# Contrast adjustment of 48 images: first tile loaded as two DMAs with two pieces per row, and stored as one

## The chip, the cores and the metric

The kernel runs on one core of one Trainium2 chip. The metric is the device time of one execution in microseconds (us); 239.36 is the median of three runs, which lie between 239.26 and 239.40. Beside the runs there is a profile of one execution, from which all times of parts come.

## The reference

```python
def setup_inputs():
    batch, c, h, w = 16, 3, 512, 512
    return {"x": np.random.rand(batch, c, h, w).astype(np.float32), "factor": np.float32(1.5)}

def reference(x, factor):
    mean = np.mean(x, axis=(2, 3), keepdims=True)
    return np.clip(mean + factor * (x - mean), 0, 1).astype(np.float32)
```

There are 48 images (16 x 3) of 512 x 512 numbers. Each gets its own mean, and every number becomes factor * x + (1 - factor) * mean, cut to between 0 and 1. All of an image has to be read before any of it can be written.

## The kernel before, in words

The 50.33 MB of input are cut into 6 tiles. A tile has 128 partitions, and each partition holds one row of ROW = 16384 numbers (64 KB), so a tile is 8 MB and holds 8 images of 16 partitions each. A buffer in on-chip memory, `ring`, has room for three tiles (BUFS = 3). Tile t uses place t % 3, and the result overwrites the input there.

For each tile, `compute` does this:

- `add` forms the sum of each row in two parts at once. VectorE (DVE) sums the first SUM = 4352 columns with a tensor_reduce (L85), and ScalarE (ACT) the rest, with a copy in place that also accumulates (L89).
- TensorE (PE) multiplies these sums with `blockw` (L100). That matrix holds (1 - factor) / 262144 where two partitions belong to the same image, so each partition gets its image's shift. The result is one column of `bias`.
- DVE computes factor * x + shift in place (L103), then the clip (L106).
- `store` writes the tile out (L80).

All loads (L77) and stores (L80) are issued by SyncE (SP), in the order in which they are written, since the schedule is by hand. They go into one DMA queue that 16 DMA engines work off. A DMA over 128 rows gives each engine 8 rows, and a packet is one contiguous piece of a row. The order on SP is: loads of tiles 0, 1 and 2; stores of tiles 0, 1 and 2; loads of 3, 4 and 5; stores of 3, 4 and 5. A store waits on SP until L106 of its tile is done, and what stands behind it on SP waits as well. Load 3 waits until store 0 has landed, since they share a place in `ring`; so do load 4 for store 1 and load 5 for store 2.

Tile 0 is treated apart. It is loaded by three DMAs: columns 0 to 2048 (1 MB), 2048 to 8192 (3 MB) and 8192 to 16384 (4 MB). Its sums are formed by halves: four partial sums instead of two, with a reduction of 4352 and an activation of 3840 columns for each half, and four products with `blockw`. Its scaling and clip are cut at column 2048, and each of the two parts has a store of its own.

Of the kernel before, what the change touches and what calls it, by code (L numbers as in the profile page):

```python
# [1 line left out]

# [4 lines left out]


P = 128  # L10
ROW = 16384
HALF = ROW // 2
BUFS = 3
SHORT = 2048
SUM = 4352


@with_exitstack
def kernel(
    ctx: ExitStack,  # L20
    tc: tile.TileContext,
    x: bass.AP,
    factor: float,
    out: bass.AP,
):

    nc = tc.nc
    f32 = mybir.dt.float32  # L30
    Alu = mybir.AluOpType
    Act = mybir.ActivationFunctionType

    B, C, H, W = x.shape
    n_img, n_pix = B * C, H * W
    ppi = n_pix // ROW
    per_tile = P // ppi
    n_tiles = n_img // per_tile
    assert ppi * ROW == n_pix and per_tile * n_tiles == n_img

    factor = float(factor)
    wconst = (1.0 - factor) / float(n_pix)

    x_f = x.rearrange("b c h w -> (b c h w)")
    out_f = out.rearrange("b c h w -> (b c h w)")

    def dram(ap, t, c0=0, c1=ROW):
        return bass.AP(tensor=ap.tensor, offset=t * P * ROW + c0, ap=[[ROW, P], [1, c1 - c0]])

    consts = ctx.enter_context(tc.tile_pool(name="consts", bufs=1))  # L50
    xpool = ctx.enter_context(tc.tile_pool(name="xpool", bufs=1))
    small = ctx.enter_context(tc.tile_pool(name="small", bufs=1))
    psum = ctx.enter_context(tc.tile_pool(name="psum", bufs=1, space=bass.MemoryType.PSUM))


    sums = small.tile([P, 4 * n_tiles], f32, name="sums")
    bias = psum.tile([P, n_tiles], f32, name="bias")

    blockw = consts.tile([P, P], f32, name="blockw")
    blocks = blockw.rearrange("p (a b) -> p a b", b=ppi)  # L60
    nc.gpsimd.memset(blockw, wconst)  # L61
    for base, step in ((0, -ppi), (ppi - 1, ppi)):
        nc.gpsimd.affine_select(  # L63
            out=blocks,
            in_=blocks,
            compare_op=Alu.is_ge,
            fill=0.0,
            base=base,
            pattern=[[step, per_tile], [0, ppi]],
            channel_multiplier=1 if step < 0 else -1,  # L70
        )


    ring = xpool.tile([P, BUFS, ROW], f32, name="ring")

    def load(t, c0=0, c1=ROW):
        nc.sync.dma_start(out=ring[:, t % BUFS, c0:c1], in_=dram(x_f, t, c0, c1))  # L77

    def store(t, c0=0, c1=ROW):
        nc.sync.dma_start(out=dram(out_f, t, c0, c1), in_=ring[:, t % BUFS, c0:c1])  # L80

    def add(t, col, c0, c1, c2):
        xt = ring[:, t % BUFS, :]
        own = sums[:, 4 * t + col : 4 * t + col + 2]
        nc.vector.tensor_reduce(  # L85
            out=own[:, 0:1], in_=xt[:, c0:c1], axis=mybir.AxisListType.X, op=Alu.add
        )
        part = xt[:, c1:c2]
        nc.scalar.activation(out=part, in_=part, func=Act.Copy, accum_out=own[:, 1:2])  # L89
        return [own[:, 1:2], own[:, 0:1]]  # L90

    def compute(t, *cuts):
        xt = ring[:, t % BUFS, :]
        if t == 0:
            parts = add(t, 0, 0, SUM, HALF) + add(t, 2, HALF, HALF + SUM, ROW)
        else:
            parts = add(t, 0, 0, SUM, ROW)
        shift = bias[:, t : t + 1]
        for k, part in enumerate(parts):
            nc.tensor.matmul(shift, blockw, part, start=k == 0, stop=k == len(parts) - 1)  # L100
        for c0, c1 in zip((0, *cuts), (*cuts, ROW)):
            part = xt[:, c0:c1]
            nc.vector.tensor_scalar(  # L103
                out=part, in0=part, scalar1=factor, scalar2=shift, op0=Alu.mult, op1=Alu.add
            )
            nc.vector.tensor_scalar(  # L106
                out=part, in0=part, scalar1=0.0, scalar2=1.0, op0=Alu.max, op1=Alu.min
            )
            store(t, c0, c1)

    with tc.manual_schedule():
        load(0, 0, SHORT)
        load(0, SHORT, HALF)
        load(0, HALF, ROW)
        load(1)
        load(2)
        compute(0, SHORT)
        compute(1)
        compute(2)
        load(3)  # L120
        load(4)
        load(5)
        compute(3)
        compute(4)
        compute(5)


# [1 line left out]
_INS = ['x', 'factor']  # L129
_OUTS = [((16, 3, 512, 512), 'float32')]  # L130

_NUMBERS = {'factor': 1.5}


# [26 lines left out]
```

## Time and profile before

| what | us |
|---|---|
| median of the runs (lowest, highest) | 239.36 (239.26, 239.40) |
| profiled execution: span, from its first to its last instruction | 237.3 |
| median of the runs less that span | 2.06 |
| DVE busy | 137.4 |
| ACT busy | 59.9 |
| PE busy | 7.9 |

The profile gives no total for the profiled execution beside its span; what lies around the span is taken as the difference to the median of the other runs.

How to read the views: in the list of groups a row gives line, engine, operation, shapes and count, then busy time and the mean of one. In the timeline the first number is the start, the second the duration, and the bracket tells how long the engine was idle before and what ended that. The row of digits headed DMA shows the busy share of the 16 DMA engines in equal slices of the window, in tenths. The queue line gives packets, megabytes and the packets' time as a share of 16 engines' span. A DMA issue is listed with its size and the time from issue to landing. The packet records of the trace, from which some durations are taken, hold start, duration and size of every packet of every DMA; a DMA's last packet on each engine has 4 bytes and reports its completion.

### The profile page before, as it was taken

The page shows a single profiled execution, that of the slowest core. Times are in us where ns is not written, and L with a number is a line of the kernel's source. Part 1 is how long each engine was busy: PE and PEld are TensorE (multiplying, and loading weights), DVE is VectorE, ACT ScalarE, POOL GpSimd, SP SyncE. Part 2 cuts the span into 40 slices and gives each one's busy share as a digit, 9 for nine tenths or more (in the row PEclk, how much of TensorE's full clock was granted, in tenths as well). Part 3 has the DMA queues.
Part 4 walks back from the last instruction along what each step waited for, and adds up shares of the span by engine and source line. Part 5 has one row for each costly group of instructions (what it writes and reads, how often), then busy time and mean ns, then how long its engine had stood idle before and what let it go on. Part 6 is the DMA issues. An engine that isn't in the chain of part 4 may idle for free.

```text
span 237.3 us, 186 instructions
## 1 busy us (share of the span) xinstructions
PE 7.9 (3%) x28; PEld 6.9 (3%) x28; DVE 137.4 (58%) x21; ACT 59.9 (25%) x15; POOL 1.1 (0%) x7
## 2 busy tenths in 40 slices
PE   0010100010001000000000000100000000000000
PEld 0010100010001000000000000100000000000000
DVE  0071899949998998000000043499989998991000
ACT  2051300980492000000000049319509800000000
POOL 1000000000000000000000000000000000000000
DMA  7999989899799798989899998989899998989894
GB/s 289 418 442 442 530 353 530 353 486 398 331 464 454 341 530 353 530 353 519 365 442 442 398 486 353 530 354 530 353 475 409 431 453 376 508 353 530 353 530 177
DMA packets 2160, 100.66 MB, mean 424 GB/s; under 512 B 240, under 2 KB 240, under 8 KB 240
## 3 DMA queue, kind: packets, MB, share of 16 engines
q1 hardware_dynamic: 2160, 100.66, 98.7%
HBM read 50.33 MB, written 50.33 MB: 424 GB/s over the span
## 4 chain that ended last, share of the span: by engine, by line
DVE 43%; DMA 36%; ACT 9%; PE 2%; SPq 1%; issue 0%; DVEq 0%; ACTq 0%
DMA ring<-in_x_dram 36%; DVE ring L103 18%; DVE ring L106 18%; ACT ring L89 9%; DVE sums L85 6%; PE bias L100 2%; SPq L77 1%; SPq L80 0%; DVEq L103 0%; ACTq L89 0%
## 5 line engine op out<-in xcount | busy, mean ns | idle before, releaser
L89 ACT ACTIVATE ring<-ring 128x12032 f32<-128x12032 f32 (+1 forms) x7 | 58.0, 8280 | 128.2 <-DMA ring<-in_x_dram 128.2
L85 DVE TENSOR_REDUCE sums<-ring 128x1 f32<-128x4352 f32 x7 | 32.8, 4683 | 63.9 <-DMA ring<-in_x_dram 63.9
L103 DVE TENSOR_SCALAR ring<-ring,bias 128x16384 f32<-128x16384 f32 (+2 forms) x7 | 52.8, 7538 | 12.9 <-PE bias L100 12.9
L106 DVE TENSOR_SCALAR ring<-ring 128x16384 f32<-128x16384 f32 (+2 forms) x7 | 52.3, 7476 | 0.2
L100 PE MATMUL bias<-sums,blockw 128*128 128x1 f32 x28 | 7.9, 360 | 189.1 <-ACT ring L89 175.4
L100 PEld LDWEIGHTS bias<-sums,blockw 128*128 128x128 f32 x28 | 6.9, 314 | 190.0 <-ACT ring L89 159.4
L89 ACT ACT_TABLE_LOAD x1 | 1.3, 1283 | 0.8 <-PEq L142 0.8
L89 ACT ACTIVATION_READ_ACCUMULATOR ring<-ring 128x1 f32 x7 | 1.3, 187 | 0.0
L63 POOL TENSOR_SCALAR_AFFINE_SELECT blockw<-blockw 128x128 f32<-128x128 f32 x2 | 0.7, 340 | 0.1
L61 POOL MEMSET blockw<- 128x128 f32 x1 | 0.2, 204 | 0.3 <-POOLq L142 0.3
L142 POOL MEMSET const-bfloat16-1.0<- 128x1 bf16 x1 | 0.1, 102 | 0.0
L142 POOL MEMSET const-uint8-127<- 128x1 uint8 x1 | 0.1, 102 | 0.0
L142 POOL MEMSET const-float32-0.0<- 128x1 f32 x1 | 0.1, 98 | 0.3 <-issue 0.3
L142 POOL MEMSET const-float32-1.0<- 128x1 f32 x1 | 0.1, 98 | 0.0
## 6 DMA issues: line engine op xcount, KB each, us to landing
out_dram<-ring SPq DMA_DIRECT2D x1, 7168.0 KB, 35.9
ring<-in_x_dram SPq DMA_DIRECT2D x1, 4096.0 KB, 20.8
ring<-in_x_dram SPq DMA_DIRECT2D x1, 3072.0 KB, 11.6
ring<-in_x_dram SPq DMA_DIRECT2D x1, 1024.0 KB, 4.7
out_dram<-ring SPq DMA_DIRECT2D x1, 1024.0 KB, 34.3
ring<-in_x_dram SPq DMA_DIRECT2D x5, 57.7
out_dram<-ring SPq DMA_DIRECT2D x5, 27.0
```

The costliest lines, as they stand in the source:

```text
L61: nc.gpsimd.memset(blockw, wconst)
L63: nc.gpsimd.affine_select(out=blocks, in_=blocks, compare_op=Alu.is_ge, fill=0.0, base=base, pattern=[[step, per_tile], [0, ppi]], channel ...
L77: nc.sync.dma_start(out=ring[:, t % BUFS, c0:c1], in_=dram(x_f, t, c0, c1))
L85: nc.vector.tensor_reduce(out=own[:, 0:1], in_=xt[:, c0:c1], axis=mybir.AxisListType.X, op=Alu.add)
L89: nc.scalar.activation(out=part, in_=part, func=Act.Copy, accum_out=own[:, 1:2])
L100: nc.tensor.matmul(shift, blockw, part, start=k == 0, stop=k == len(parts) - 1)
L103: nc.vector.tensor_scalar(out=part, in0=part, scalar1=factor, scalar2=shift, op0=Alu.mult, op1=Alu.add)
L106: nc.vector.tensor_scalar(out=part, in0=part, scalar1=0.0, scalar2=1.0, op0=Alu.max, op1=Alu.min)
L142: nc = _bacc.Bacc("TRN2", target_bir_lowering=False, num_devices=1)
```

## The change

Tile 0 is now loaded by two DMAs. Each takes, from every row, one piece of both halves: the first takes columns 0 to 2048 and 8192 to 10240 (two pieces of 8 KB), the second 2048 to 8192 and 10240 to 16384 (two pieces of 24 KB). Each of the 16 DMA engines so gets 16 packets from each of the two. Tile 0 is then computed like every other tile: one reduction of 4352 columns, one activation of 12032, two products, one scaling and one clip over the whole row, and one store. The order of loads and stores of the tiles stays as it was. The numbers of the lines move: L85 becomes L92, L103 and L106 become L105 and L108, the stores' L80 becomes L87, and the two loads of tile 0 stand in L84.

```diff
-SHORT = 2048
+SHORT = ROW // 8
...
-    sums = small.tile([P, 4 * n_tiles], f32, name="sums")
+    sums = small.tile([P, 2 * n_tiles], f32, name="sums")
...
+    def load_first(c0, c1):
+        rows = bass.AP(
+            tensor=x_f.tensor, offset=c0, ap=[[ROW, P], [HALF, 2], [1, c1 - c0]]
+        )
+        halves = ring[:, 0, :].rearrange("p (a b) -> p a b", a=2)
+        nc.sync.dma_start(out=halves[:, :, c0:c1], in_=rows)
...
-    def compute(t, *cuts):
+    def compute(t):
         xt = ring[:, t % BUFS, :]
-        if t == 0:
-            parts = add(t, 0, 0, SUM, HALF) + add(t, 2, HALF, HALF + SUM, ROW)
-        else:
-            parts = add(t, 0, 0, SUM, ROW)
+        parts = add(t, 0, SUM, ROW)
...
-        for c0, c1 in zip((0, *cuts), (*cuts, ROW)):
-            part = xt[:, c0:c1]
-            nc.vector.tensor_scalar(
-                out=part, in0=part, scalar1=factor, scalar2=shift, op0=Alu.mult, op1=Alu.add
-            )
-            nc.vector.tensor_scalar(
-                out=part, in0=part, scalar1=0.0, scalar2=1.0, op0=Alu.max, op1=Alu.min
-            )
-            store(t, c0, c1)
+        nc.vector.tensor_scalar(
+            out=xt, in0=xt, scalar1=factor, scalar2=shift, op0=Alu.mult, op1=Alu.add
+        )
+        nc.vector.tensor_scalar(
+            out=xt, in0=xt, scalar1=0.0, scalar2=1.0, op0=Alu.max, op1=Alu.min
+        )
...
-        load(0, 0, SHORT)
-        load(0, SHORT, HALF)
-        load(0, HALF, ROW)
-        load(1)
-        load(2)
-        compute(0, SHORT)
-        compute(1)
-        compute(2)
-        load(3)
-        load(4)
-        load(5)
-        compute(3)
-        compute(4)
-        compute(5)
+        for first in range(0, n_tiles, BUFS):
+            turn = range(first, min(first + BUFS, n_tiles))
+            for t in turn:
+                if t == 0:
+                    load_first(0, SHORT)
+                    load_first(SHORT, HALF)
+                else:
+                    load(t)
+            for t in turn:
+                compute(t)
+                store(t)
```

More of the change, by code (lines that the diff above doesn't have):

```diff
@@ L11 @@
 ROW = 16384
+BUFS = 3
+SUM = 4352
 HALF = ROW // 2
-BUFS = 3
-SHORT = 2048
-SUM = 4352
+SHORT = ROW // 8
 @with_exitstack
@@ L77, in load, with add @@
         nc.sync.dma_start(out=ring[:, t % BUFS, c0:c1], in_=dram(x_f, t, c0, c1))
+    def load_first(c0, c1):
[4 more added lines that the diff above has]
+        nc.sync.dma_start(out=halves[:, :, c0:c1], in_=rows)
     def store(t, c0=0, c1=ROW):
         nc.sync.dma_start(out=dram(out_f, t, c0, c1), in_=ring[:, t % BUFS, c0:c1])
-    def add(t, col, c0, c1, c2):
+    def add(t, c0, c1, c2):
         xt = ring[:, t % BUFS, :]
-        own = sums[:, 4 * t + col : 4 * t + col + 2]
+        own = sums[:, 2 * t : 2 * t + 2]
         nc.vector.tensor_reduce(
```

## The prediction

> **What bounds the kernel now.** I read the page's queue line first, then the chain of waits, then the waits of SP, then the timeline of the first three tiles, and last the DMA activity in narrow windows.
>
> ```profile
> span 237.3 us, 186 instructions
> PE 7.9 (3%) x28; PEld 6.9 (3%) x28; DVE 137.4 (58%) x21; ACT 59.9 (25%) x15; POOL 1.1 (0%) x7
> DMA  7999989899799798989899998989899998989894
> q1 hardware_dynamic: 2160, 100.66, 98.7%
> ```
>
> The queue line is the one to see: there is one queue, and its packets fill 98.7% of the span on all 16 engines. No compute engine is above 58%. The chain of waits gives DVE 43% and DMA 36%, which would mislead here: it follows instructions back, and SP's instructions wait for DVE before they are issued.
>
> ```profile
> SPq L80 <- DVE ring L106: 181.8, 7, 47.8
> SPq L77 <- DMA out_dram<-ring: 25.6, 2, 19.3
> ```
>
> SP does wait 181.8 us for DVE, but each store it then issues joins a queue that is not empty. The DMA issues show it: a store needs far longer to land than its own data needs.
>
> ```profile
> out_dram<-ring SPq DMA_DIRECT2D x1, 7168.0 KB, 35.9
> out_dram<-ring SPq DMA_DIRECT2D x1, 1024.0 KB, 34.3
> ```
>
> The 1 MB store takes 34.3 us to land because two whole loads stand before it. So the kernel is one unbroken line of transfers: tiles 0, 1, 2 in, 0, 1, 2 out, 3, 4, 5 in, 3, 4, 5 out. What counts is the sum of the packets' times and any moment at which the line runs dry.
>
> Every DMA ends, on each engine, with a completion packet of 4 bytes. By the packet records of the trace the earliest of the 16 begins at 4.79, 12.06 and 21.74 us for the three loads of tile 0, at 41.06 and 61.40 for tiles 1 and 2, at 63.85 and 80.76 for the two stores of tile 0, then at 100.08, 119.40, 138.72, 158.04, 177.48, 196.79, 216.11 and 235.43. The differences are the prices: 7.27 us for a DMA of 24 KB rows, 9.68 for 32 KB rows, 2.45 for 8 KB rows (61.40 to 63.85, without the start of the run), 16.91 for 56 KB rows, 19.32 for a whole tile of 64 KB rows, read or written. The next DMA's first packet begins about 6 ns after the completion packet.
>
> **The change, part by part.**
>
> *First load.* Before: 2.45 + 7.27 + 9.68 = 19.40 us of queue. After: 16 packets of 8 KB per engine instead of 8, so 2 x 2.45, and 16 of 24 KB, so 2 x 7.27: 19.44. That is +0.04 us. I assume that a packet of 8 or 24 KB costs the same when its neighbour in the row lies 32 KB away; the bounds on that are in the next paragraph and in the rivals.
>
> *Start of the queue.* The first load is issued at 0.80 us and its first packet begins at 1.82, 1.02 us later; the 16 engines begin within 0.32 us of each other. The first DMA now has 256 pieces instead of 128. The five loads at the start are issued 0.46 us apart, so 128 pieces need at most 0.46 us. Lower end: 0, if the first packets go out while later pieces are still made (one could even gain the 0.32 us of spread if the pieces are dealt out differently, though nothing points there). Upper end: +1.02, if the whole lead doubles. I take 0, because SP's loads and stores, with rows from 8 to 64 KB, differ by more among themselves (327 to 622 ns to issue a load) than a count of pieces explains, and keep both ends. The second DMA's pieces are made beneath 4.9 us of the first one's packets.
>
> *First store.* Before 2.45 + 16.91 = 19.36 (61.40 to 80.76); after one DMA of 64 KB rows, 19.32: -0.04 us.
>
> *Later compute of tile 0.* This part looks costly and should cost nothing. Before, tile 0 is summed in halves and its first 1 MB is stored at 30.5 us:
>
> ```profile
> 12.86 3.40 ACT L89 ACTIVATE ring<-ring 128x3840 f32<-128x3840 f32 x1 [10.78 <-DMA ring<-in_x_dram]
> 22.58 3.40 ACT L89 ACTIVATE ring<-ring 128x3840 f32<-128x3840 f32 x1 [6.22 <-DMA ring<-in_x_dram]
> 30.41 7.68 DVE L103 TENSOR_SCALAR ring<-ring,bias 128x14336 f32<-128x14336 f32 x1
> 41.93 10.23 ACT L89 ACTIVATE ring<-ring 128x12032 f32<-128x12032 f32 x1 [15.86 <-DMA ring<-in_x_dram]
> 53.43 8.76 DVE L103 TENSOR_SCALAR ring<-ring,bias 128x16384 f32<-128x16384 f32 x1 [3.07 <-PE bias L100]
> ```
>
> After, both sums start when all of tile 0 is there, 22.58 + 0.04 = 22.62. A whole tile needs 11.50 us from ACT's start to L103 (41.93 to 53.43), then 17.48 for L103 and L106 (53.43 to 70.91): done at 51.60, store 0 issued at 51.7. DVE then sums tile 1: from the end of one tile to its next L103 it takes 5.35 (70.91 to 76.26), so L103 begins at 56.95 instead of 53.43, and store 1 goes out at 74.5 instead of 71.0. Tile 2 needs 22.85 (70.91 to 93.76): store 2 at 97.4 instead of 93.8, with load 3 right behind it on SP. With the 1.02 us lead the queue can take them at 52.7, 75.5 and 98.4. It asks for them when the transfer ahead ends: 61.40, 80.76 and 100.08. The margins are 8.7, 5.3 and 1.7 us; without this cover each microsecond too late would be one lost. Load 3 is asked for at 119.40, load 4 waits for store 1 (100.08) and load 5 for store 2, as before. So nothing from tile 3 on moves, and SP is not held on anything new: its wait for store 0 now has one DMA instead of two.
>
> *Fewer instructions.* One reduction, one activation, two matmul pairs and two tensor_scalar go. DVE, ACT and PE are off the path, so they give nothing.
>
> **Sum:** +0.04 - 0.04 + 0 = 0.00 us on the profiled span of 237.3. The median of the runs is 239.36, that is 2.06 us around the span, which no part of the change touches. Forecast 239.36.
>
> **The rivals.**
>
> *Faster: a stall goes with the small store.* One stretch of the line is too long: tile 2's load takes 20.34 us (41.06 to 61.40), all others 19.32 to 19.44. The packet records put it in the last packet of that load, on all 16 engines: 3.53 us on average instead of 2.42. At the second change from loads to stores (tile 5 to store 3) the last packets take 2.54. The DMA view in slices of 0.4 us shows both, first from 54 to 70 us, then from 172 to 188:
>
> ```profile
> DMA  0003900005900000002799999930039900099000
> ```
>
> ```profile
> DMA  0993000993000999000799000799000799000799
> ```
>
> Digits stand where packets end. In the first row the bursts come 2.4 us apart until 58 us, and the next one only after 61; in the second the beat goes on. What differs ahead of the stall is that an 8 KB store waits in the queue in the first case and a 64 KB one in the second. If that makes the stall, the change removes 3.53 - 2.54 = 0.99 us: 238.4. Against it: no store packet has begun yet, 8 KB and larger loads follow each other at the start without such a stall, and the first case is also the first write of the run at all, which the change keeps. The first read of the run is slow too (first packets 0.83 us instead of 0.31). I think the first write is the likelier owner: chance 0.25.
>
> *Faster: completions paid in series.* The last completion packets begin at 236.07 us at the latest and the span ends at 237.3, so a store's completion may cost up to 1.2 us; two DMAs fewer would then give 237.0 to 239.4. The 6 ns to the next DMA's packet speak against it: chance 0.02. The Trainium skill, "DMA: Bandwidth & Descriptors", section "Anatomy of one DMA — SWDGE (gpsimd) path", fits a fixed 2.0 us to each DMA of another issuing path; taken twice that would give 235.4. The trace disagrees for DMAs that stand in line.
>
> *Slower: the first load starts later.* If a DMA's first packet waits until all its pieces are made, 256 pieces lengthen the lead of 1.02 us by 0.46 (the issue spacing) up to 1.02, and since the line is never idle afterwards the end moves as much: 239.8 to 240.4, middle 240.1. It counts as slower from 0.48 us. For it: nothing hides the first 1.82 us. Against it: engines begin 0.32 us apart, so packets already go out one by one. Chance 0.13.
>
> *Slower: store 2 comes too late*, if DVE or ACT lose more than the 1.7 us of margin: 239.36 plus the overrun, for example 240.4. DVE's whole-tile operations repeat to 0.01 us, so 0.03. *The change does not do what it says*, the pieces go to few engines (two engines would need some 155 us for tile 0): the outer count is still 128, so 0.01.
>
> **How the numbers follow.** A difference under 0.2% (0.48 us) cannot be told from none. Same 0.56 (239.36, its own range 239.2 to 239.8 by half of the start's bound), faster 0.25 + 0.02 = 0.27, slower 0.13 + 0.03 + 0.01 = 0.17. The range has to reach the stall's case, 238.4 less 0.2 of spread, and the lower half of the later start: 238.2 to 239.9, which leaves out about 0.17.
>
> **What would show it.** Right: tile 0's completion packets end near 21.8 us, ACT waits for DMA until 22.6, store 0 is issued at 51.7 and lands near 82, and the stall before the first store is still 1.1 us. The stall's rival: a 64 KB last packet of load 2 near 2.5 us. The later start: a first packet after 2.2 us. Store 2 late: an empty slice near 99 us. Wrong altogether: 8 or 24 KB packets that are not 0.31 and 0.91 us long.

## The result, and the profile after

The changed kernel takes 242.01 us (median of four runs, 241.72 to 242.60), the kernel before 239.38 us beside it (239.26 to 239.53). The ratio is 1.011, with a 95% interval of 1.0098 to 1.0122: 2.63 us slower, where 239.36 was forecast. The profiled execution has a span of 240.4 us.

The page's lines that answer to those shown of before:

```profile
span 240.4 us, 169 instructions
PE 6.7 (3%) x24; PEld 5.9 (2%) x24; DVE 132.5 (55%) x18; ACT 63.2 (26%) x13; POOL 1.1 (0%) x7
DMA  6999989899898989898998989898999989898984
q1 hardware_dynamic: 2128, 100.66, 98.0%
```

The same bytes and a queue that is nearly as full, over a longer span. SP's waits do not explain it either:

```profile
SPq L87 <- DVE ring L108: 183.8, 6, 49.1
SPq L77 <- DMA out_dram<-ring: 20.7, 2, 19.4
SPq L87 <- DMA ring<-in_x_dram: 5.2, 1, 5.2
```

The last row is new, but it is a wait for tile 0's first load that ends at 8.5 us, long before store 0 is issued at 53.59. The packet records show where the time goes. The table sets the last completion packets of both traces side by side, for the slowest of the 16 engines, since the slowest sets the end.

| completion packet of | before, us | after, us | after less before |
|---|---|---|---|
| tile 0's load | 22.15 | 22.68 | +0.53 |
| load 2 (then the change to stores) | 62.02 | 62.36 | +0.34 |
| store 1 | 100.70 | 101.00 | +0.30 |
| store 2 (then the change to loads) | 120.02 | 120.78 | +0.76 |
| load 3 | 139.40 | 141.09 | +1.69 |
| load 4 | 158.72 | 160.41 | +1.69 |
| load 5 (then the change to stores) | 178.11 | 181.09 | +2.98 |
| store 5, the end | 236.07 | 239.05 | +2.98 |

So 0.30 us is left of a later start, and 2.7 us come at two changes of direction long after tile 0: from store 2 to load 3, and from load 5 to store 3. Between them nothing is lost; whole tiles take 19.32 us in both traces. The DMA activity shows it in slices of 0.4 us. First the kernel before, from 112 to 128 us:

```profile
DMA  9900009900009930009930009930009970009970
```

Then the changed kernel, from 112 to 128 us and from 172 to 188:

```profile
DMA  0990000990000990000099040039907039737009
```

```profile
DMA  3307973309995500099703399703399333399333
```

In the kernel before, the packets end in bursts 2.4 us apart all along. In the changed kernel's first row this beat breaks near 120 us: the third pause is longer, and afterwards single engines trail behind the burst. From 172 to 188 us the kernel before was regular too (shown with the prediction). In the changed kernel's second row the bursts are already spread out at its left end, there is a long pause near 178 us, and the trailing gets worse.

What is late ahead of the first of these places is store 2. The timeline of the changed kernel:

```profile
23.19 1.28 ACT L96 ACT_TABLE_LOAD   x1 [23.19 <-DMA ring<-in_x_dram]
24.48 10.23 ACT L96 ACTIVATE ring<-ring 128x12032 f32<-128x12032 f32 x1
36.04 8.76 DVE L105 TENSOR_SCALAR ring<-ring,bias 128x16384 f32<-128x16384 f32 x1 [8.14 <-PE bias L104]
99.28 0.33 SPq L87 DMA_DIRECT2D out_dram<-ring  x1
```

And of the kernel before, where the table load and store 2 stood:

```profile
0.80 1.28 ACT L89 ACT_TABLE_LOAD   x1 [0.80 <-PEq L142]
93.82 0.33 SPq L80 DMA_DIRECT2D out_dram<-ring  x1
```

ACT loads its function table before its first activation. In the kernel before that stands ahead of any wait and is done at 2.1 us. In the changed kernel the first activation waits for two DMAs; in ACT's instructions, in the order of the program, one of the two waits stands ahead of the table load and the other on the activation. So 1.28 us that used to be free stand on the path, and store 2 is issued at 99.28 us, 1.1 us before store 1's first completion packet at 100.41.

### The profile page after: what moved, and what is told of

It is laid out like the page before. It is cut to its first block, busy times and chain, and to the rows that moved or that the text cites. A ratio compares the mean times of both kernels' runs of the same rounds, so it can differ in the third digit from the quotient of the medians.

```text
span 240.4 us, 169 instructions
## 1 busy us (share of the span) xinstructions
PE 6.7 (3%) x24; PEld 5.9 (2%) x24; DVE 132.5 (55%) x18; ACT 63.2 (26%) x13; POOL 1.1 (0%) x7
## 4 chain that ended last, share of the span: by engine, by line
DVE 51%; DMA 26%; ACT 9%; PE 2%; issue 1%; SPq 0%; DVEq 0%; ACTq 0%
DMA ring<-in_x_dram 26%; DVE ring L105 22%; DVE ring L108 22%; ACT ring L96 9%; DVE sums L92 8%; PE bias L104 2%; ACT L96 1%; SPq L84 0%; SPq L87 0%; DVEq L105 0%; ACTq L96 0%
## 5 line engine op out<-in xcount | busy, mean ns | idle before, releaser
L96 ACT ACTIVATE ring<-ring 128x12032 f32<-128x12032 f32 x6 | 61.4, 10230 | 105.4 <-DMA ring<-in_x_dram 105.4
L92 DVE TENSOR_REDUCE sums<-ring 128x1 f32<-128x4352 f32 x6 | 28.1, 4681 | 65.5 <-DMA ring<-in_x_dram 65.5
L105 DVE TENSOR_SCALAR ring<-ring,bias 128x16384 f32<-128x16384 f32 x6 | 52.5, 8757 | 18.0 <-PE bias L104 18.0
L108 DVE TENSOR_SCALAR ring<-ring 128x16384 f32<-128x16384 f32 x6 | 52.2, 8694 | 0.2
L104 PE MATMUL bias<-sums,blockw 128*128 128x1 f32 x24 | 6.7, 360 | 191.9 <-ACT ring L96 171.0
L104 PEld LDWEIGHTS bias<-sums,blockw 128*128 128x128 f32 x24 | 5.9, 314 | 192.6 <-ACT ring L96 136.5
L96 ACT ACT_TABLE_LOAD x1 | 1.3, 1283 | 23.2 <-DMA ring<-in_x_dram 23.2
```

The source lines that it names most:

```text
L92: nc.vector.tensor_reduce(out=own[:, 0:1], in_=xt[:, c0:c1], axis=mybir.AxisListType.X, op=Alu.add)
L105: nc.vector.tensor_scalar(out=xt, in0=xt, scalar1=factor, scalar2=shift, op0=Alu.mult, op1=Alu.add)
L108: nc.vector.tensor_scalar(out=xt, in0=xt, scalar1=0.0, scalar2=1.0, op0=Alu.max, op1=Alu.min)
```

## The experiments

Theory L: the stalls come from issuing store 2 only about a microsecond before it is needed, although the packets of store 1 and store 2 follow each other without a gap. "Need" is here the first completion packet of the DMA ahead. Rival S: the shape of the first load makes the stalls. Rival W: the single first store does. A time "beside" another is beside the kernel before on the same chip. How far ahead a DMA was issued is read from the one execution that was profiled.

**Each part of the change alone.** The two-piece loads alone, in the kernel before:

```diff
+    def load_first(c0, c1):
...
-        load(0, 0, SHORT)
-        load(0, SHORT, HALF)
-        load(0, HALF, ROW)
+        load_first(0, SHORT)
+        load_first(SHORT, HALF)
```

> The kernel before with only the two loads of tile 0 in two pieces per row; sums by halves, two cuts and two stores of tile 0 stay. Theory S (the shape of the first load does it: a later start of 0.57 us and later stalls at the changes of direction): 241.5 to 242.3, with last packets of store 2 and load 5 of 2.9 us and more. Theory L (tile 0's later compute does it, through the late store 2): 239.7 to 240.0, that is before plus the start alone, since the table load stays at 0.8 us and tile 0 is done earlier than in the changed kernel. Theory W (one 8 MB first store instead of 1 + 7 MB): also 239.7 to 240.0.

Measured: 239.72 us beside 239.34, ratio 1.0017 (1.0008 to 1.0025). The new load costs some 0.4 us, and the last packets of store 2 are regular. S falls.

The single store alone:

```diff
-            store(t, c0, c1)
+        store(t)
```

> The kernel before with only the store of tile 0 made one DMA; it is issued when both parts are clipped, near 45.8 us. Theory W: 241.0 to 242.0, with the start as before. Theories L and S: 239.2 to 239.5, the same as before.

Measured: 239.61 us, ratio 1.0013 (1.0003 to 1.0023), so it costs 0.1 to 0.6 us and not 2. W falls. With a store of 64 KB packets waiting in the queue, the last packets of load 2 are still 1.34 us over their usual length on average (1.11 in the kernel before). That also settles the forecast's rival: the stall at the first change has nothing to do with the 8 KB store.

Compute and store of the changed kernel, loads of the kernel before:

```diff
-        if t == 0:
-            parts = add(t, 0, 0, SUM, HALF) + add(t, 2, HALF, HALF + SUM, ROW)
-        else:
-            parts = add(t, 0, 0, SUM, ROW)
+        parts = add(t, 0, 0, SUM, ROW)
...
-        compute(0, SHORT)
+        compute(0)
```

> The kernel before, its three loads of tile 0 kept, with the compute and the single store of the changed kernel; the activation table is loaded late here too, near 22.5 us. Theory L: 241 to 242, with stalls at store 2 to load 3 and load 5 to store 3. Theory W: 241 to 242 as well. Theory S: 239.2 to 239.6.

Measured: 240.34 us, ratio 1.0042 (1.0022 to 1.0061), with runs from 239.52 to 241.88. In the profiled execution, one of the faster ones (239.88), store 2 is issued 1.5 us before its need (98.73 against 100.21). The runs scatter between nothing and the full loss, which fits a threshold near that margin.

**The changed kernel with the table loaded early:**

```diff
+    warm = consts.tile([P, 1], f32, name="warm")
+    nc.gpsimd.memset(warm, 0.0)
+    nc.scalar.activation(out=warm, in_=warm, func=Act.Copy)
```

> The changed kernel with one tiny activation on a 128x1 tile at the start, so that the activation table is loaded near 0.8 us and not at 23.2; all that follows on ACT and DVE for tiles 0 to 2 comes 1.3 us earlier and store 2 is issued near 98.0 instead of 99.3. Theory L: 239.8 to 240.3, the stalls at the later changes of direction go and only the later start is left. Theories S and W: 241.6 to 242.3, no change.

Measured: 239.88 us beside 239.34, ratio 1.0025 (1.0015 to 1.0036). One instruction of 0.2 us takes back about four fifths of the loss. Its timeline:

```profile
0.80 1.28 ACT L76 ACT_TABLE_LOAD   x1 [0.80 <-PEq L144]
2.09 0.20 ACT L76 ACTIVATE warm<-warm 128x1 f32<-128x1 f32 x1
23.15 10.23 ACT L100 ACTIVATE ring<-ring 128x12032 f32<-128x12032 f32 x1 [20.86 <-DMA ring<-in_x_dram]
```

and its DMA activity from 112 to 128 us, where the beat goes on through the change of direction at 120:

```profile
DMA  0999000999000999000999000999000999000999
```

The Trainium skill, "ScalarE: Activation LUTs", section "What ACT_TABLE_LOAD costs", calls the load an instruction of the engine itself and gives about 1283 ns for it. The trace agrees on the 1.28 us; that a wait can land on it is what decided here.

**The late store alone, in the kernel before:**

```diff
+    junk = small.tile([P, 2], f32, name="junk")
...
+        if t == 2:
+            for k, n in enumerate((SUM, 768)):
+                nc.vector.tensor_reduce(
+                    out=junk[:, k : k + 1], in_=xt[:, 0:n], axis=mybir.AxisListType.X, op=Alu.add
+                )
```

> The kernel before with two extra reductions of tile 2 on DVE (4352 and 768 columns, into a column that nothing uses), so that store 2 and load 3 behind it are issued 5.5 us later, near 99.3 and 99.7 us, as in the changed kernel; loads and stores are otherwise as before. Theory L (store 2 and load 3 that come within about a microsecond of the queue's need make stalls at the changes of direction): 240.0 to 242.0, scattered by a microsecond, with packets over 2.6 us around 117 and 176 us. Rival (those stalls need the new first load as well, or belong to the chip on which the changed kernel ran): 239.2 to 239.5.

Measured: 241.87 us beside 239.38, ratio 1.0109 (1.0094 to 1.0123), as much as the whole change. Store 2 is issued 1.2 us before its need (99.18 against 100.35). DMA activity from 112 to 128 us:

```profile
DMA  0970000990000990000099300099390039390039
```

The beat breaks at the same place as in the changed kernel, with the old loads and the old first stores. Theory L holds, and no part of the change is needed for the loss.

**Load 3 alone late:**

```diff
+        nc.vector.memset(ring[:, 0, 0:10240], 0.0)
         load(3)
```

> The kernel before with a memset by DVE of 10240 columns of tile 0's place in the ring after tile 2, which load 3 must wait for: load 3 alone is issued late, near 99.7, while store 2 goes out at 93.8 as before. If it is load 3's issue that counts (its descriptors come when store 2 has begun or is about to): 240.0 to 242.0 with the stall at store 2 to load 3. If it is store 2's: 239.2 to 239.5.

Measured: 239.50 us, ratio 1.0004 (0.9995 to 1.0012). Load 3 went out at 104.58 us, later still than planned, and nothing was lost: its need is at 119.76. So it is not load 3's lateness behind store 2 that counts.

**A small store early in the run:**

```diff
+    tiny = consts.tile([P, 128], f32, name="tiny")
...
         load(0, 0, SHORT)
+        nc.sync.dma_start(out=dram(out_f, 5, 0, 128), in_=tiny)
```

> The kernel before with an extra store of 64 KB (512 bytes a row, zeros into the place that store 5 overwrites at the end) behind the first load, so that the first write of the run happens near 5 us. If the 1.1 us in the last packets of load 2 belong to the first write of the run, they leave 60 us and come back, in part or whole, near 5 us: 238.6 to 239.6, with a last packet of load 2 near 2.5 us. If they belong to the change from loads to large stores at that place, the last packets stay near 3.5 us and the extra store adds 0.2 to 1.2 us: 239.6 to 240.6.

Measured: 241.18 us beside 239.38, ratio 1.0067 (1.0055 to 1.0079). The first change of direction still costs 0.86 us on average. The stall there is not the price of the first write. The extra 1.8 us were more than expected; in the trace two engines fall about 0.7 and 1.3 us behind the others right after the small store and stay behind. Why they do is open.

**The changed kernel again**, on the chip of the three runs just above:

> The changed kernel itself, on the chip of this group. Theory L: 241 to 242.6, some scatter between runs, since store 2 is issued about 1.1 us ahead of need on any chip. Rival (the first chip was special): near 240.0, as with the early table load.

Measured: 241.58 us beside 239.38, ratio 1.0083 (1.0059 to 1.0107), runs from 240.39 to 242.46. In this trace store 2 is issued 1.4 us before its need (99.13 against 100.53), and the loss is there all the same.

**Old loads with the new compute, the single store and the early table:**

> The three loads of tile 0 of the kernel before with the whole-tile compute and single store of the changed kernel, and the tiny activation that loads the table early; store 2 near 97.3 us, about 2.8 us ahead of need. If the table's place and the first load's shape are all there is: 239.2 to 239.6, the same as before. If the later compute or the single store cost something besides: 239.8 or more.

Measured: 239.50 us beside 239.47, ratio 1.0000 (0.9992 to 1.0009). Store 2 is issued at 97.25, 3.3 us ahead. The later compute and the single store are free, as forecast, once the table load is out of the way. This version is simpler than the kernel before and as fast; none of the versions was faster.

**How late is late.** The expectations from here on call it theory R that a DMA issued just before its need costs the engines a lead with which they read ahead, so that the next change of direction has to wait. First a smaller delay in the kernel before (`(3136, 768)` in place of `(SUM, 768)`), then a larger one (`(SUM, 3232)`):

> The kernel before with extra reductions of 3136 and 768 columns on DVE ahead of tile 2 (4.2 us): store 2 is issued near 98.0 us, 2.1 us ahead of need, still 1.1 us more than the first packet's lead of 1.02. Theory R with a threshold at that lead: 239.3 to 239.6. A cost that grows evenly with lateness from 93.8 on: about 241.2, three quarters of the way to the late case.

Measured: 239.44 us beside 239.47, ratio 1.0001 (0.9992 to 1.0009); issued 2.2 us ahead (98.35 against 100.55):

```profile
98.35 0.33 SPq L81 DMA_DIRECT2D out_dram<-ring  x1
```

> The kernel before with extra reductions of 4352 and 3232 columns on DVE ahead of tile 2 (8.2 us): store 2 is issued near 102.0 us, after the queue has run empty near 100.1 to 100.7. Theory R: an open gap of 102.0 + 1.0 - 100.4 = 2.6 us, and behind it the same stalls as in the late case (2.4 us): 243.5 to 245. If the stalls are another form of the gap: 241.9 to 242.6, the gap alone.

Measured: 243.19 us, ratio 1.0153 (1.0140 to 1.0166). The queue runs dry (the completion packets come at 100.58 to 101.07, the next packets begin at 102.55 to 102.70). On average over the engines that gap is 1.84 of the 3.72 us; the other 1.9 are longer packets, nearly all of them at the same two changes of direction. So the stalls come on top of the gap.

**The same at another place of the queue.** Load 4 is held back by memsets into its place in the ring. The first version held it too long, the second (64 columns in place of 9792) too short, the third has 2048:

```diff
+        for n in (ROW, ROW, 9792):
+            nc.vector.memset(ring[:, 1, 0:n], 0.0)
         load(4)
```

> The kernel before with memsets by DVE into tile 1's place of the ring while DVE would idle, so that load 4 is issued near 137.5 us, about 1.2 us before load 3 ends, instead of 101.5; store 2 and load 3 stay early. Theory R (a DMA issued just before its need costs the engines the lead with which they read ahead, and the next change of direction then has to wait): the last packets of load 5, before store 3, rise from 2.54 to 3 us and more and the run takes 239.9 to 241.5. Theory that only store 2, ahead of the change back to loads, is sensitive: 239.2 to 239.6.

Measured: 248.93 us, ratio 1.0393 (1.0380 to 1.0407). The memsets had idle time ahead of each, so load 4 went out at 145.99, and the queue stood empty for over 7 us. It says nothing of a load that is only just late, but the next change of direction, load 5 to store 3, took 1.1 us more than a tile's 19.32, where the kernel before loses 0.13.

> As the late load 4, with the third memset cut to 64 columns, so that load 4 is issued near 137.8 us, about 1.1 us before load 3 ends, without a dry queue. Theory R: packets stay back to back at 139 us, the last packets of load 5 before store 3 rise from about 2.6 to 3 us and more, 239.9 to 241.0. Theory that only a late store or a dry queue costs: 239.2 to 239.7.

Measured: 239.63 us beside 239.54, ratio 1.0001 (0.9991 to 1.0011). Load 4 went out at 135.74, 3.1 us ahead of need; no loss, and no answer.

> As the late load 4 again, with a third memset of 2048 columns, timed by what the memsets took in the two runs before (1.05 ns a column with the idle time ahead of each): load 4 is issued near 137.7 us, about 1.1 us before load 3 ends. Theory R: no gap at 139 us, but the step from load 4 to load 5 (completion packets), which takes in the change to store 3, rises from 19.4 to 19.8 us in earlier runs to 20.1 us and more, and the run takes 239.9 to 241.0. Theory that only a late store or a dry queue costs: 239.3 to 239.7.

Measured: 241.92 us beside 239.50, ratio 1.0100 (1.0081 to 1.0118). Here load 4 goes out as late as was meant:

```profile
136.28 1.76 DVE L122 MEMSET ring<- 128x2048 f32 x1 [0.49 <-DVE ring L122]
138.07 0.81 SPq L77 DMA_DIRECT2D ring<-in_x_dram  x2
```

Load 4 is issued at 138.07, 1.1 us before load 3's first completion packet at 139.13. On most engines its packets begin at once, on three only at 140.36 to 140.97, when load 3's last completion packet came at 139.73. Its first packets are 2.4 to 3.7 us long, and on average load 4 takes 0.86 us more than a tile's 19.32. The change to store 3 then costs another 1.1 us on average, and from 172 to 188 us, where the kernel before was regular, there is a long pause near 178:

```profile
DMA  0300990300990600009970039990039990039990
```

So it is not a property of store 2. The runs scatter from 240.99 to 243.48, and the profiled one is the slowest of them.

**More pieces**, the changed kernel with the early table and four pieces per row:

```diff
-            tensor=x_f.tensor, offset=c0, ap=[[ROW, P], [HALF, 2], [1, c1 - c0]]
+            tensor=x_f.tensor, offset=c0, ap=[[ROW, P], [HALF // 2, 4], [1, c1 - c0]]
...
-                    load_first(0, SHORT)
-                    load_first(SHORT, HALF)
+                    load_first(0, SHORT // 2)
+                    load_first(SHORT // 2, HALF // 2)
```

> The changed kernel with the early table load, and with four pieces per row in each of the two first loads (4 and 12 KB, 512 pieces in a DMA). If the start is delayed by each piece (0.39 us for 128 more): first packet near 3.0 us instead of 2.2, and 240.6 to 241.2. If the delay belongs to the two-dimensional form and not to the count: first packet near 2.2, and 239.8 to 240.1.

Measured: 242.02 us beside 239.54, ratio 1.0100 (1.0086 to 1.0114). The first packet begins at 2.21 us, as with two pieces (2.21) and later than with one (1.82): the 0.39 us belong to the two-dimensional form, not to the count. The time is still worse, since the small first packets run slowly, tile 0 arrives 2 us later, and store 2 comes too late again.

## Why the prediction was wrong, point by point

- *The bound* and the *prices of the packets* were right. The queue line reads 98.0%; the 24 KB load took 14.54 us, twice 7.27, and tile 0's store 19.32.
- *Start of the queue*: taken as 0, it was a later first packet by 0.39 us, within the bounds of 0 to 1.02. In this trace the first packets were also slower (1.02 us on average instead of 0.83), and tile 0's load ended 0.53 us later; in the other three traces of this load all its packets together lose no more than in the kernel before (0.49 to 0.54 us beyond their usual length, 0.60 before). The rival of a later start, given 0.13, so had the effect right but not the reason: it does not go by the count of pieces, as the four pieces showed. The parts with this load and without the stalls cost 0.38 (load alone) and 0.54 us (early table).
- *Later compute of tile 0* is the step that failed, twice. First, the table load was not counted among the things that move: L105 of tile 0 began at 36.04, not 34.12, of which 1.28 are the table and 0.6 the later load. The margin of 1.7 us that the text gave store 2, after the 1.02 us lead, became about 0.1. Second, and worse, "each microsecond too late would be one lost" was the wrong rule. Nothing was too late by it, and 2 us were lost. The runs put in its place: 2.2 us or more between issue and need cost nothing, 1.5 us sometimes, 1.1 to 1.4 us some 2.2 to 2.6 (in the two measurements of the changed kernel about 0.4 of it is the later start).
- *Rival, store 2 too late*: the right place, given 0.03, with a price (the overrun) that was wrong for the same reason.
- *Rival, small store*: refuted by the single store. The owner that I preferred, the first write, is refuted by the early small store.
- *Completions in series*: one DMA fewer gave no gain (the old loads with early table: ratio 1.0000), and two fewer did not either (the changed kernel with early table: 1.0025).

**What the stalls are** is shown in their effect and argued in their cause. Added up over all packets of tiles 0 to 2's loads, the time beyond each size's usual length is 1.63 to 2.08 us per engine in all 17 traces, but it is spread differently: 0.60 at the start and 1.11 at the first change of direction in the kernel before, 1.69 and 0.01 with four pieces. Later changes are nearly free in the kernel before (0.02 and 0.13). After a late issue nearly the same is lost once more: 1.4 us in both traces of the changed kernel, 1.5 for the late store alone, 1.9 behind the dry queue and 1.8 for load 4, where a part of it falls on load 4's own first packets. A short lead does no harm by itself: store 5 of the kernel before goes out at 214.64, 1.5 us before its need at 216.11, and each of its packets takes the usual 2.42 us, but no change of direction comes after it. All of this looks like a lead that an engine's reading has over its writing. It is paid for once after a start, then hides the change of direction, and is lost when the next DMA is not there yet for the reading side, even if the writing side still has work. The Trainium skill, "DMA: Bandwidth & Descriptors", section "Two DMAs through the same engine are not ordered", says that an engine's read and write sides are separate queues, which fits; the packet records here show one line per engine, so the lead itself was not seen. That the loss in time (2.2 to 2.6 us) is larger than the average stall (1.4 to 1.8) fits the spread: the engines end 2.1 us apart in the changed kernel, 0.64 before, and the slowest counts.

## What to carry to other kernels

In a kernel that is bound by one DMA queue, a packet line without gaps is not enough: see by how much each DMA's issue is ahead of the end of the transfer before it, and do not be content with the 1.02 us from issue to first packet: here 1.4 us ahead was too little and 2.2 us was enough. When a first instruction gets another wait, look at what stands right before it on its engine, since one-time work such as the table load can move behind that wait. And price a loss where it appears, from one stage to the next, because these 2.7 us appeared 20 and 80 us after their cause.

## What the runs showed of the hardware

- A DMA issued 1.1 to 1.4 us before the first completion packet of the one ahead cost 2.2 to 2.6 us. For store 2 this came at the next changes of direction and not at its own start; for load 4 a part came at its own start. 2.2 us ahead cost nothing.
- A load with two or four pieces per row sends its first packet 1.41 us after issue, with one piece per row 1.02; with 4 KB pieces the first DMA's completions spread over 1.6 us instead of 0.4.
- From one DMA to the next in the line there are 6 ns, and a packet of 8 to 64 KB takes 0.31 to 2.42 us, that is its bytes at 27 GB/s per engine and a few ns.
